# A recurrence's outputs in one run of products per half, and four transfers that the planner treats as independent

## The chip, the cores and the metric

One core of a Trainium2 chip. The time is that of one execution of the whole program in microseconds on the device; the figure of a kernel is the median of its runs. A core has four compute engines that the profile names PE (matrix products; PEld are its weight loads), DVE, ACT and POOL, and SP, which only issues transfers here. They run on their own and meet at semaphores.

## The reference, cut to what matters

A block of an encoder over 1024 positions of width 1024, in float32: a normalised input goes through one wide projection `h @ w_in`, whose columns feed two branches (stick-breaking attention and an RWKV-7 recurrence), then sigmoid gates, an output projection, and a SwiGLU FFN. The change lies in the recurrence. For each of 8 heads of 64 channels it is

```python
def step(state, inp):
    r_t, w_t, k_t, v_t, kk_t, a_t = inp
    sa = jnp.einsum('bhvk,bhk->bhv', state, -kk_t)
    state = (state * w_t[:, :, None, :]
             + sa[..., None] * (kk_t * a_t)[:, :, None, :]
             + v_t[..., None] * k_t[:, :, None, :])
    return state, jnp.einsum('bhvk,bhk->bhv', state, r_t)
```

over the positions, and its outputs `y` are normalised per head, get a bonus term and are gated.

## The kernel before, in words

**Tiling.** The recurrence works on pairs of heads (4 pairs, 128 rows: one head in rows 0 to 63, the other in 64 to 127) and on halves of 512 positions, so there are eight (pair, half) units. A half is cut into 8 chunks of 64 positions. `rw_elementwise` makes what each chunk needs: `ar` (decayed keys and queries), `bk`, and `nx`, two tiles of four chunks each that hold products of `bk` and `ar` under a mask; these are the 64-row products `e_e<-b_ar,b_bk`. `rw_inverse` inverts the triangular part of all chunks of a half at once: DVE works off 31 steps of forward substitution in tile `ts` (class `q`), then four transfers write every fourth row of `ts` to a DRAM scratch `td` (lines 1033 and 1034), one transfer reads `td` back in another order (`dt`, line 1036), and 32-row products on PE finish it. `rw_chain` walks through the 8 chunks: a product with `nx` and the state `sv` (tile `c`, `c_c<-b_sv,b_nx`), two copies into `xv`, a product with `bkt` (`c_c<-b_xv,b_bkt`), and two operations that make the next state in `sv`. After chunk 3 and after chunk 7 it makes the outputs of the four chunks past: 8 products of 64 rows and 64 columns (`y_y<-b_ar,b_sv`) and 8 of 128 rows and 64 columns (`y_y<-b_nx,b_xv`) into one PSUM tile `y`. `rw_post` copies `y` out, normalises, gates and stores it.

**What else PE has meanwhile.** The projections of the next pair (`project`) and the sigmoid gates (`gate_tiles`), 128-row products into tile `d` (`d_d<-big_h,whi_whi` and `d_d<-big_h,wlo_wlo`); the gates come with the lowest priority, wherever there is room. After the recurrence come attention, the merge, the output projection and the FFN, which are products of full size.

**The order.** No line issues an instruction directly. Every operation is recorded with a priority (its place in the program, moved by offsets: the chain comes 1000 places ahead, the inverse 300, gates 10 million behind) and with the operations that it depends on, found from overlapping regions. A planner, `schedule`, then plays the program through with estimated costs (`cost`) and latencies (`LATENCY`: 2030 ns from one transfer to an operation that needs it) and writes out one fixed order for each engine. In it:

- `choose` picks PE's next operation among those that are ready. Normally that is the one of highest priority; after a product whose cost is under 70 it takes another of cost under 70 if one is ready. `array_mode` gives a product's share of the PE array: its contraction rows and its columns, each rounded up to 32, 64 or 128.
- `together()` makes products a bundle, which is issued in one piece once all of its operations can go.
- Tiles lie in pools with a fixed number of places: `y` has 2 places of PSUM, `c`, `d` and `e` 2 each, `b` 27 places in SBUF. A tile takes a place when the planner grants it and gives it back after its last reader.
- Two transfers to the same DRAM tensor whose regions seem to overlap depend on each other for the planner. The regions of the four `td` transfers interleave, and `regions` describes them by their outer span.

All instructions are issued at line 579, so the profile's rows are told apart by their tiles.

## Time and profile before

| | |
|---|---|
| median of 3 runs | 1610.81 us (1609.73 to 1612.65) |
| profiled execution | 1610.57 us, span 1608.8 us |
| PE busy | 1586.0 us, 99% of the span |
| DVE, ACT, POOL busy | 1128.0, 716.5, 254.5 us |
| granted PE clock | 0.999 |
| recurrence's first and last `td` transfer | 152.9 and 463.4 us |
| recurrence's first and last output product | 185.9 and 507.9 us or just after |

The span is the time from the first to the last instruction; the execution's own time has some work around it besides. Rows of groups read: engine, operation, tile written and tiles read, shape, count, busy time, mean ns of one, idle time of the engine before them. Rows in order of time read: start, length, engine, operation, tiles, shape, count, and in brackets the engine's idle time and what ended it. Rows of waits read: who waited for whom, us in total, times, the longest. Matmuls are pipelined: their lengths overlap, and what one costs is the distance between starts.

### The profile page before, as it was taken

To read this page: it belongs to the slowest core of one execution; us is meant where nothing else is said; L and a number is where in the kernel's file an instruction comes from. 1 tells how busy PE (TensorE), PEld (TensorE's weight loads), DVE (VectorE), ACT (ScalarE), POOL (GpSimd) and SP (SyncE) were. 2 spreads that over 40 slices of the span, in tenths; PEclk is the share of its full clock that TensorE was granted. 3 is DMA by queue.
4 is the path that set the end of the run, shared out by engine and by line. 5 is a ranking of instruction groups with operands and counts; after the bars stand their busy time and mean duration, and the time that the engine had idled before them with its cause. 6 is when DMAs were issued, how large, how long until landed. Compare 5 with 4: busy or idle time off the path is not lost.

```text
span 1608.8 us, 23912 instructions
## 1 busy us (share of the span) xinstructions
PE 1586.0 (99%) x8932; PEld 1284.1 (80%) x8932; DVE 1128.0 (70%) x2004; ACT 716.5 (45%) x1401; POOL 254.5 (16%) x407
## 2 busy tenths in 40 slices
PE   9999999999999999999999999999999999999998
PEld 7877777777787888888787888888888888888876
DVE  7568689897864878895366349766666666867485
ACT  7533345444245766774444334323332332554352
POOL 1030233525233222230043110000000000000000
PEclk9999999999999999999999999999999999999999
DMA  5523233242321000003537112332232233874444
GB/s 214 203 88 92 79 100 86 59 140 83 105 71 40 27 27 27 27 27 122 180 118 274 66 40 81 116 98 98 99 111 89 95 111 124 310 240 144 136 152 183
DMA packets 106822, 180.38 MB, mean 112 GB/s; under 512 B 42321, under 2 KB 43345, under 8 KB 106706
## 3 DMA queue, kind: packets, MB, share of 16 engines
q1 hardware_dynamic: 106706, 178.85, 33.6%
q8 instruction: 70, 1.15, 0.3%
q14 instruction: 46, 0.38, 0.1%
HBM read 129.27 MB, written 47.45 MB: 110 GB/s over the span
## 4 chain that ended last, share of the span: by engine, by line
PE 86%; DVE 7%; ACT 3%; DMA 3%; issue 1%; POOL 0%; SPq 0%; DVEq 0%; ACTq 0%; POOLq 0%
PE d_d L579 39%; PE e_e L579 20%; PE c_c L579 16%; PE y_y L579 10%; DVE q_q L579 2%; DVE b_sv L579 1%; DMA b_wraw<-w_fd 0%; DVE big_h L579 0%; DVE b_xs L579 0%; ACT b_qst L579 0%; DMA q_q<-td 0%; DVE wlo_wlo L579 0%; DMA whi_oraw<-w_o 0%; DMA b_g<-gsc 0%; DVE b_nx L579 0%
## 5 line engine op out<-in xcount | busy, mean ns | idle before, releaser
L579 PE MATMUL d_d<-big_h,whi_whi 128*128 128x512 f32 x1280 | 434.5, 409 | 0.1
L579 PEld LDWEIGHTS d_d<-big_h,whi_whi 128*128 128x128 f32 x1280 | 234.9, 189 | 48.7 <-issue 5.5
L579 PE MATMUL d_d<-big_h,wlo_wlo 128*128 128x512 f32 x640 | 259.9, 406 | 0.0
L579 PEld LDWEIGHTS d_d<-big_h,wlo_wlo 128*128 128x128 f32 x640 | 120.7, 189 | 24.6 <-issue 2.4
L579 DVE TENSOR_TENSOR q_q<-b_nl,q_q 128x2 f32<-128x2 f32 (+30 forms) x248 | 86.5, 349 | 9.9 <-POOL b_sh L579 2.4
L579 ACT CAST whi_whi<-raw_raw 128x1024 fp32r<-128x1024 f32 (+1 forms) x60 | 55.9, 933 | 77.5 <-PE d_d L579 76.4
L579 DVE TENSOR_TENSOR_SCAN b_nb<-b_nb 128x128 f32<-128x128 f32 (+3 forms) x64 | 87.9, 1390 | 1.7 <-POOL b_nb L579 1.0
L579 DVE TENSOR_TENSOR wlo_wlo<-raw_raw,whi_whi 128x1024 fp32r<-128x1024 f32 (+1 forms) x60 | 69.5, 1160 | 27.4 <-ACT whi_whi L579 27.3
L579 POOL TENSOR_SCALAR sp_sp<-b_sv,pl_pl 64x64 f32<-64x64 f32 x120 | 63.3, 528 | 121.9 <-DVE b_sv L579 115.9
L579 ACT CAST b_wd<-b_wraw 128x512 fp32r<-128x512 f32 x70 | 42.1, 620 | 64.4 <-DVE b_wraw L579 30.0
L579 DVE TENSOR_REDUCE q_q<-q_q 128x1 f32<-128x2 f32 (+30 forms) x248 | 62.1, 250 | 6.8
L579 PE MATMUL d_d<-b_wd,big_act 128*128 128x512 f32 x264 | 66.5, 395 | 0.0
L579 PE MATMUL e_e<-b_wd,big_act 128*128 128x512 f32 x264 | 66.5, 394 | 0.0
L579 DVE TENSOR_TENSOR b_wd<-b_wraw,b_wd 128x512 fp32r<-128x512 f32 x70 | 46.4, 686 | 27.0 <-ACT b_wd L579 27.0
L579 POOL TENSOR_SCALAR_AFFINE_SELECT b_nb<-b_nb 128x128 f32<-128x128 f32 x64 | 45.4, 716 | 123.5 <-ACT b_nb L579 108.4
L579 PEld LDWEIGHTS e_e<-b_wd,big_act 128*128 128x128 f32 x264 | 49.6, 188 | 11.8
L579 PEld LDWEIGHTS d_d<-b_wd,big_act 128*128 128x128 f32 x264 | 49.6, 188 | 11.7
L579 DVE TENSOR_TENSOR b_wt<-c_c,b_wt 128x512 fp32r<-128x512 f32 (+2 forms) x96 | 50.0, 546 | 3.8 <-ACT b_wt L579 2.7
L579 ACT CAST b_wt<-c_c 128x512 fp32r<-128x512 f32 (+2 forms) x96 | 43.5, 481 | 20.5 <-PE c_c L579 19.5
L579 ACT COPY b_xv<-c_c 64x64 f32<-64x64 f32 x64 | 13.3, 207 | 86.2 <-DVE b_xv L579 46.0
L579 PE MATMUL c_c<-b_wd,big_act 128*128 128x512 f32 x198 | 50.8, 395 | 0.1
L579 PE MATMUL y_y<-b_wd,big_act 128*128 128x512 f32 x198 | 50.7, 394 | 0.0
(648 smaller groups left out, 3576.4 us busy)
## 6 DMA issues: line engine op xcount, KB each, us to landing
raw_raw<-w_in SPq DMA_DIRECT2D x42, 512.0 KB, 3.5
raw_raw<-w_fg SPq DMA_DIRECT2D x22, 512.0 KB, 3.5
raw_raw<-w_fu SPq DMA_DIRECT2D x22, 512.0 KB, 3.6
b_wraw<-w_fd SPq DMA_DIRECT2D x22, 512.0 KB, 4.7
act<-b_u SPq DMA_DIRECT2D x39, 256.0 KB, 3.1
b_x<-x SPq DMA_DIRECT2D x16, 512.0 KB, 9.0
b_mg<-gsc SPq DMA_DIRECT2D x28, 256.0 KB, 5.3
raw_araw<-act SPq DMA_DIRECT2D x14, 512.0 KB, 4.5
```

Of the source, the lines that this page charges most:

```text
L579: getattr(getattr(self.real, op.engine), op.method)(**kw)
```

## The change

Three edits. (1) `choose`: the rule "after a short one, another short one" goes by the array's contraction rows (under 128) in place of the estimated cost (under 70). (2) `rw_inverse`: the four transfers to `td` are taken out of each other's dependencies; the read of `td` still depends on all four. (3) `rw_chain`: the outputs of all eight chunks of a half are made in one bundle behind the last chunk (16 products of the one kind, then 16 of the other), where there were two bundles of 8 and 8, behind chunk 3 and chunk 7.

```diff
-        if able[0][2].engine == "tensor" and last is not None and last.cost < 70:
-            short = [x for x in able if x[2].cost < 70]
+        if able[0][2].engine == "tensor" and last is not None and array_mode(last)[0] < P:
+            short = [x for x in able if array_mode(x[2])[0] < P]
...
     td = b.scratch([32, 8, 4, 32], f"td{p}{hf}")
+    stores = set()
     for c in range(4):
         nc.sync.dma_start(td[:, :, c, :], ts[c:P:4])
+        b.ops[-1].preds -= stores
+        stores.add(b.ops[-1])
...
-        if c % 4 == 3:
-            g = c // 4
-            if y is None:
-                y = u["y"] = T("y", [P, H])
-            with b.together():
-                for k in range(4 * g, c + 1):
-                    for h, rs in hs:
-                        nc.tensor.matmul(y[rs, k * CH : k * CH + CH], lhsT=sv[rs, k, rs], rhs=ar[rs, k, CH:P], start=k == 0, stop=False, skip_group_check=True)
-                for k in range(4 * g, c + 1):
-                    for h, rs in hs:
-                        nc.tensor.matmul(y[rs, k * CH : k * CH + CH], lhsT=xv[:, k, rs], rhs=nx[g][:, k % 4, 1, h, :], start=False, stop=k == 7, skip_group_check=True)
+    y = u["y"] = T("y", [P, H])
+    with b.together():
+        for k in range(8):
+            for h, rs in hs:
+                nc.tensor.matmul(y[rs, k * CH : k * CH + CH], lhsT=sv[rs, k, rs], rhs=ar[rs, k, CH:P], start=k == 0, stop=False, skip_group_check=True)
+        for k in range(8):
+            for h, rs in hs:
+                nc.tensor.matmul(y[rs, k * CH : k * CH + CH], lhsT=xv[:, k, rs], rhs=nx[k // 4][:, k % 4, 1, h, :], start=False, stop=k == 7, skip_group_check=True)
```

## The prediction

> **What bounds the kernel now.** First the head of the page, its busy times and the engines' shares of the chain that ended last.

> ```profile
> span 1608.8 us, 23912 instructions
> ## 1 busy us (share of the span) xinstructions
> PE 1586.0 (99%) x8932; PEld 1284.1 (80%) x8932; DVE 1128.0 (70%) x2004; ACT 716.5 (45%) x1401; POOL 254.5 (16%) x407
> ...
> PE 86%; DVE 7%; ACT 3%; DMA 3%; issue 1%; POOL 0%; SPq 0%; DVEq 0%; ACTq 0%; POOLq 0%
> ```

> PE has work for 1586.0 of 1608.8 us and makes 86% of the chain. So a gain has to come out of PE's own stream: fewer products, less time lost between them, or fewer waits of PE. A result that is ready sooner on another engine is worth nothing unless PE stood waiting for it. Second, two stretches side by side: the recurrence (130 to 520) and the dense stretch of the FFN (960 to 1400).

> ```profile
> core 0: us, PE busy (x) PEld busy (x) DVE busy (x) ACT busy (x) POOL busy (x), PEclk, DMA share, GB/s
> 130.00:520.00 390.00, 384.02 (x3218) 303.75 (x3217) 308.95 (x833) 162.91 (x354) 126.92 (x239) 1.00 0.30 86
> 960.00:1400.00 440.00, 440.00 (x1906) 356.88 (x1905) 304.70 (x454) 146.64 (x234) 0.00 (x0) 1.00 0.34 115
> ```

> In the recurrence PE is without work for 390.00 - 384.02 = 6.0 us. The change touches nothing after it, and the granted clock is 1.00 in both. Third, what PE waited for there, the two largest rows:

> ```profile
> PE c_c L579 <- DVE b_sv L579: 2.2, 5, 0.7
> PE c_c L579 <- ACT b_xv L579: 1.4, 3, 0.6
> ```

> Both are steps of the serial chain over the chunks, and short (0.7 us at most). Otherwise projections and gates (tile d) fill PE while the chain, the inverse or a transfer is under way. That fill is the cover for everything below that I cost at nothing.

> **The outputs of a half in one run.** No product is added or removed; two runs of 16 products become one of 32, and one run's changes of array shape go. Fourth view: PE in order of time around a first run (start, length, operation, count), and the groups by shape.

> ```profile
> 184.19 0.38 PE L579 MATMUL c_c<-b_sv,b_nx 128*128 128x128 f32 x2
> 184.33 0.71 PE L579 MATMUL d_d<-big_h,whi_whi 128*128 128x512 f32 x2
> 184.88 0.39 PE L579 MATMUL d_d<-big_h,wlo_wlo 128*128 128x512 f32 x1
> 185.11 0.63 PE L579 MATMUL d_d<-big_h,whi_whi 128*128 128x512 f32 x2
> 185.58 0.38 PE L579 MATMUL c_c<-b_xv,b_bkt 128*128 128x128 f32 x2
> 185.89 0.68 PE L579 MATMUL y_y<-b_ar,b_sv 64*64 64x64 f32 x16
> 186.50 0.69 PE L579 MATMUL y_y<-b_nx,b_xv 128*64 128x64 f32 x16
> 187.12 0.50 PE L579 MATMUL d_d<-big_h,wlo_wlo 128*128 128x512 f32 x1
> 187.46 0.38 PE L579 MATMUL c_c<-b_sv,b_nx 128*128 128x128 f32 x2
> ```
> ```profile
> L579 PE MATMUL y_y<-b_nx,b_xv 128*64 128x64 f32 x256 | 11.0, 228 | 0.0
> L579 PE MATMUL y_y<-b_ar,b_sv 64*64 64x64 f32 x256 | 10.9, 224 | 0.0
> L579 PE MATMUL e_e<-b_ar,b_bk 64*128 64x128 f32 x192 | 13.9, 285 | 0.0
> ```

> A float32 product stands as two passes: 256 passes of each kind in runs of 16 are 16 runs, two for each of the eight halves. Starts are read, since lengths overlap.
> - From the chain's product at 185.58 to the next one at 187.46 pass 1.88 us: that product, the run, one d product.
> - Without the run: c to d takes 184.33 - 184.19 = 0.14. The d product after a c takes 0.55 (184.33 to 184.88, two of them) less the usual 0.23 (184.88 to 185.11) = 0.32. Together 0.46.
> - So a run costs 1.88 - 0.46 = 1.42 us.
> - Its pace: 16 passes of one kind take 0.68 from first start to last end and one lasts 0.224, so 15 steps take 0.456, 0.030 each. Sixteen more passes are 0.49 us, both kinds 0.97.
> - Doubling one run therefore costs 0.97 and saves the other's 1.42: 0.45 a half, over eight halves **3.6 us off PE's stream**.

> I take 3.6. Every first run has whole-array work on both sides in the trace, so no change of shape was shared there. [...]

> [...]

> What moves with it: the outputs of chunks 0 to 3 leave their place ahead of chunk 4's first product, which can start up to 1.4 us sooner, and come instead ahead of the next half's first product and of the normalisation, about 1.0 us later there. Fill covers both; without that cover it is eight times the difference, about 3 us either way. On POOL, DVE, ACT and SP nothing is added.

> Held longer: the first nx tile of the "b" pool (27 places), now until the second run's time. Held shorter: the y place. In the same half the second run begins 12.3 us after the first (185.89 to 198.19), and the copy that frees y comes just behind it:

> ```profile
> 198.19 0.68 PE L579 MATMUL y_y<-b_ar,b_sv 64*64 64x64 f32 x16
> 198.80 0.69 PE L579 MATMUL y_y<-b_nx,b_xv 128*64 128x64 f32 x16
> ```
> ```profile
> 199.61 0.59 ACT L579 COPY b_gg<-y_y 128x512 f32<-128x512 f32 x1 [1.96 <-POOL b_ar L579]
> ```

> So y is held for 14.3 us (185.89 to 200.20) now and for some 3 us after; the next half's inverse has both y places to itself meanwhile. I put this at nothing: PE's waits name neither place.

> **The choice of the next product.** After a product with under 128 contraction rows the planner now takes another such one; so far this was after products with an estimate under 70. Outputs end in a 128-row product (128*64 above) and lose the rule; the 64*128 products (192 passes, 12 runs here) gain it. Lost: at three places the outputs are followed directly by another run of part-array products, two of them of this form:

> ```profile
> 389.97 0.69 PE L579 MATMUL y_y<-b_nx,b_xv 128*64 128x64 f32 x16
> 390.58 0.33 PE L579 MATMUL y_y<-b_bkt,b_tmp 64*64 64x64 f32 x4
> ```

> A neighbour saves an exit (187.12 to 187.46 is 0.34 against 0.23: 0.11) and an entry (185.58 to 185.89 is 0.31 against 0.14: 0.17), 0.28 us. So the loss is at most 0.8. The gain is at most 12 x 0.28 = 3.4, if after every 64*128 run another is ready. I take 0: ready neighbours are rare, and the gain and loss are of a size.

> **The four stores.** SyncE's issues around one inverse, and around the one where nothing stood between:

> ```profile
> 340.72 1.22 SPq L579 DMA_DIRECT2D td<-q_q  x2
> 343.60 0.33 SPq L579 DMA_DIRECT2D orw<-b_ptmp  x1
> 344.99 0.33 SPq L579 DMA_DIRECT2D gsc<-b_tmp  x1
> 345.36 0.52 SPq L579 DMA_DIRECT2D td<-q_q  x1
> 347.79 0.33 SPq L579 DMA_DIRECT2D raw_raw<-w_in  x1
> 348.17 0.52 SPq L579 DMA_DIRECT2D td<-q_q  x1
> ...
> 351.55 0.37 SPq L579 DMA_DIRECT2D q_q<-td  x1
> ```
> ```profile
> 460.53 3.45 SPq L579 DMA_DIRECT2D td<-q_q  x4
> ```
> ```profile
> DMA to landing us min/median/max: 1.9/2.4/3.9
> ```

> On the chip the stores never waited for each other (two in 1.22 us, four in 3.45): what the planner took for a dependence only spread them over the queue, behind stores that wait for POOL or ACT and a weight load that waits for its buffer. In one row they take 4 x 0.6 = 2.4 us, plus a landing of 2.4, so the read goes out 4.8 us after the first store instead of 351.55 - 340.72 = 10.8: about 6 us sooner, eight times. What they move past on SP (weight loads, gate and output stores) is issued up to 1.8 us later. ACT's cast of the weights covers that:

> ```profile
> ACT whi_whi L579 <- PE d_d L579: 31.5, 15, 6.7
> ```

> It waits for PE to give a buffer back, not for the load. Late next after the inverse is the chain, under PE's fill. I put the stores at 0; the bounds are a loss of 1.8 us for one load laid bare and a gain of the 6.0 us that PE stands idle.

> **Sum.** 1610.57 (the profiled execution, 1.8 over its span and 0.24 under the median of the runs) - 3.6 + 0 + 0 = 1607.0, or 1607.2 on the median's scale.

> **Rivals.**
> - *The plan gives it back.* Every priority is renumbered and the four stores have new times, so the order changes over the whole recurrence; 3.6 us is five or six waits of 0.6 us. For: the chain's waits depend on what happens to stand in front on DVE, which is 79% busy there (308.95 of 390). Against: inverses that end sooner leave the planner more room, not less. Time 1609.5 to 1612, about 1610.6.
> - *PE's waits go too.* If inverses 6 us sooner and a free y place let the plan keep chain and fill apart, the 6.0 us of idle PE vanish: 1607.2 - 6.0 = 1601.2; half of them, 1604.2. Against: the waits named are on DVE and ACT in the chain, which no store feeds. [...]
> - *Slower: the nx place.* One place of 27 stays taken for 12.3 us more in each half. If the pool is full then, a projection's output gets no place, its PSUM tile is not drained and the fill stops. For: the pool holds nearly everything of the recurrence. Against: the page has 0.1 us of idle time before the d products of most gates and projections (the last number of the row).

> ```profile
> L579 PE MATMUL d_d<-big_h,whi_whi 128*128 128x512 f32 x1280 | 434.5, 409 | 0.1
> ```

>   One such hold laid bare costs 12.3: 1607.2 + 12.3 = 1619.5. It decides the sign from 3.6 us on, and a measurable loss from 6.8 us, 1614.0.

> **How the numbers follow.** A measurement of this kernel tells 0.2% (3.2 us) from no change: faster is below 1607.6, slower above 1614.0. The sum as it stands gets 0.45, with a range of its own from 1605.5 to 1609; some six in ten of it lie below 1607.6. The plan gives it back 0.23; waits go too 0.18 (of which the reading by weight loads 0.03); the nx place 0.14. So faster 0.28 + 0.18 = 0.46, same 0.17 + 0.23 = 0.40, slower 0.14. The range runs from 1602.0, into the second rival, to 1613.0, over the first; it leaves out the slower case and the lowest part of the second, 0.19.

> **What would show it.** Right: eight runs of 32 and 32 passes of outputs, each about 2.4 us from first start to the next product, and none with 16; q_q<-td issued about 5 us after the first td; PE's idle time between 130 and 520 still near 6 us; the stretch from the merge on as long as before. Wrong: PE waits on b_sv, b_xv or q_q that sum to 3 us more or less than now, a d product that waits, or a gap at the end of attention, where the planner's order could also differ.

## The result and the profile after

The changed kernel takes 1614.74 us (median of 14 runs, 1610.9 to 1620.07) against 1610.87 us (14 runs, 1608.89 to 1613.04) before: ratio 1.0023, 95% interval 1.0015 to 1.0031. It is 3.9 us slower where 3.6 us of gain were forecast. The profiled execution took 1613.99 us. The head of its page and the engines' shares of the chain:

```profile
span 1612.2 us, 23902 instructions
## 1 busy us (share of the span) xinstructions
PE 1586.4 (98%) x8932; PEld 1281.9 (80%) x8932; DVE 1125.0 (70%) x2004; ACT 715.8 (44%) x1401; POOL 258.3 (16%) x407
...
PE 83%; DVE 8%; DMA 3%; issue 2%; ACT 1%; POOL 1%; SPq 0%; DVEq 0%; POOLq 0%; ACTq 0%
```

PE has the same 1586 us of work, and 3.4 us more of span around it. The two stretches of the prediction:

```profile
core 0: us, PE busy (x) PEld busy (x) DVE busy (x) ACT busy (x) POOL busy (x), PEclk, DMA share, GB/s
130.00:520.00 390.00, 380.50 (x3195) 297.17 (x3195) 304.64 (x830) 162.18 (x351) 132.32 (x239) 1.00 0.30 85
960.00:1400.00 440.00, 440.00 (x1905) 356.62 (x1904) 303.71 (x453) 147.49 (x236) 1.45 (x1) 1.00 0.33 114
```

In the recurrence PE stands without work for 390.00 - 380.50 = 9.5 us, where it was 6.0. The dense stretch is unchanged: from the first product of the merge to the end both traces take 848.9 us (759.9 to 1608.8, and 763.3 to 1612.2). What PE waited for between 130 and 530, all rows:

```profile
PE y_y L579 <- DVE q_q L579: 5.2, 5, 1.4
PE e_e L579 <- DVE b_nx L579: 1.8, 4, 0.8
PE c_c L579 <- ACT b_xv L579: 0.9, 1, 0.9
PE c_c L579 <- DVE b_xv L579: 0.8, 2, 0.4
```

The chain's waits on b_sv (2.2 us before) are gone. In their place PE waits 5.2 us in five places, up to 1.4 us each, for DVE to hand it the transposed read of `td`: the first 32-row run of an inverse. In the kernel before, that row was

```profile
PE y_y L579 <- DVE q_q L579: 1.0, 2, 0.7
```

The waits on q_q come from the inverse's transfers, which got *faster*. Here is one inverse, SyncE's issues and DVE's transpose behind them:

```profile
337.10 2.53 SPq L579 DMA_DIRECT2D td<-q_q  x4
339.73 0.55 SPq L579 DMA_DIRECT2D gsc<-b_tmp  x1
343.17 0.38 SPq L579 DMA_DIRECT2D q_q<-td  x1
```
```profile
345.56 0.45 DVE L579 STREAM_TRANSPOSE q_q<-q_q 128x256 f32<-128x256 f32 x1 [2.02 <-DMA q_q<-td]
```

The four stores go in 2.53 us and the transpose starts 345.56 - 337.10 = 8.5 us after the first. In the kernel before it was 355.68 - 340.72 = 15.0 us at the same inverse:

```profile
355.68 0.44 DVE L579 STREAM_TRANSPOSE q_q<-q_q 128x256 f32<-128x256 f32 x1
```

But the planner counts 0.45 us for each store and 2.03 until it has landed, and gives the transpose 6.8 us after the first store (from 332.35 to 339.13 in its own plan). Over the eight inverses the changed plan puts it 6.4 to 7.1 us behind the first store, and on the chip it starts between 0.2 us sooner and 1.7 us later than that, 0.7 us later in the mean. In the kernel before the plan had 12.5 to 14.3 us, and the chip was between 0.4 us sooner and 0.8 us later. PE's order is fixed by the plan, and PE in order of time shows what follows:

```profile
344.27 0.40 PE L579 MATMUL d_d<-big_h,wlo_wlo 128*128 128x512 f32 x1
346.07 0.69 PE L579 MATMUL y_y<-q_q,b_nx 32*32 32x32 f32 x32 [1.40 <-DVE q_q L579]
346.69 0.81 PE L579 MATMUL d_d<-big_h,whi_whi 128*128 128x512 f32 x2
347.30 0.63 PE L579 MATMUL d_d<-big_h,wlo_wlo 128*128 128x512 f32 x1
347.73 0.63 PE L579 MATMUL d_d<-big_h,whi_whi 128*128 128x512 f32 x1
348.15 0.63 PE L579 MATMUL c_c<-b_sv,b_nx 128*128 128x128 f32 x2
```

The products behind the 32-row run belong to the same tile d, and read the same kinds of operands, as those ahead of it. They could have gone first, but the order puts them behind, and PE waits 1.40 us. Then a second cost: the d products behind it last 0.63 us, 0.43 apart (347.30 to 347.73), not 0.39 and 0.23. The windows around it give the granted clock:

```profile
343.80:347.20 3.40, 2.00 (x38) 1.43 (x37) 1.55 (x2) 2.17 (x4) 1.12 (x1) 1.00 0.45 116
347.20:350.60 3.40, 3.40 (x10) 2.73 (x10) 1.06 (x3) 1.18 (x4) 1.35 (x4) 0.50 0.68 228
350.60:354.00 3.40, 3.40 (x44) 2.57 (x44) 0.33 (x3) 1.07 (x3) 0.00 (x0) 1.00 0.04 17
```

After a stretch in which PE worked 2.00 of 3.40 us, the clock is 0.50 for 3.4 us, which costs half of it, 1.7 us. Over the runs of the changed kernel the mean granted clock goes from 0.999 in the fastest (1610.9 us) to 0.994 in the slowest (1620.1). One such stretch takes 1.7/1612 = 0.001 off the mean, so by this estimate the number of stretches differs from run to run, and with it the time.

The long run of outputs does what it should. PE around the first one, and the groups by shape between 130 and 520:

```profile
191.47 0.41 PE L579 MATMUL c_c<-b_xv,b_bkt 128*128 128x128 f32 x2
191.81 1.15 PE L579 MATMUL y_y<-b_ar,b_sv 64*64 64x64 f32 x32
192.89 1.15 PE L579 MATMUL y_y<-b_nx,b_xv 128*64 128x64 f32 x32
193.97 0.50 PE L579 MATMUL d_d<-big_h,wlo_wlo 128*128 128x512 f32 x1
194.31 0.40 PE L579 MATMUL d_d<-big_h,whi_whi 128*128 128x512 f32 x1
```
```profile
L579 PE MATMUL y_y<-b_nx,b_xv 128*64 128x64 f32 x256 | 9.2, 225 | 0.0
L579 PE MATMUL y_y<-b_ar,b_sv 64*64 64x64 f32 x256 | 9.2, 221 | 0.0
```

From the c product to the d product after the next is 194.31 - 191.47 = 2.84 us; less the 0.46 of the c and d themselves a long run costs 2.38 us, against 2.39 forecast and 2 x 1.42 for two short ones: 3.7 us less over eight halves. So of the 3.4 us of span: 3.7 gained in the outputs, 3.5 lost in idle PE, 1.7 to the half clock, 0.4 before the recurrence (the first 64-row run starts at 110.57 in place of 110.14; the changed kernel's profile has a stretch of half clock at 33.2, that of before has none there). The remaining 1.5 us I cannot assign.

### The profile page after: what moved, and what is told of

Read it like the earlier page. It is cut to its first block, busy times and chain, and to the rows that moved or that the text cites. A ratio compares the mean times of both kernels' runs of the same rounds, so it can differ in the third digit from the quotient of the medians.

```text
span 1612.2 us, 23902 instructions
## 1 busy us (share of the span) xinstructions
PE 1586.4 (98%) x8932; PEld 1281.9 (80%) x8932; DVE 1125.0 (70%) x2004; ACT 715.8 (44%) x1401; POOL 258.3 (16%) x407
## 4 chain that ended last, share of the span: by engine, by line
PE 83%; DVE 8%; DMA 3%; issue 2%; ACT 1%; POOL 1%; SPq 0%; DVEq 0%; POOLq 0%; ACTq 0%
PE d_d L579 37%; PE e_e L579 19%; PE c_c L579 17%; PE y_y L579 11%; DVE q_q L579 3%; DVE b_nx L579 1%; DVE b_sv L579 1%; DVE b_bk L579 1%; DMA b_nl<-nd 1%; DMA q_q<-td 1%; SPq L579 0%; DVE wlo_wlo L579 0%; DMA whi_oraw<-w_o 0%; DMA b_mg<-gsc 0%; DVE big_h L579 0%
## 5 line engine op out<-in xcount | busy, mean ns | idle before, releaser
L579 PE MATMUL d_d<-big_h,whi_whi 128*128 128x512 f32 x1280 | 434.6, 409 | 0.3
L579 PEld LDWEIGHTS d_d<-big_h,whi_whi 128*128 128x128 f32 x1280 | 235.5, 189 | 48.9 <-issue 5.6
L579 PE MATMUL d_d<-big_h,wlo_wlo 128*128 128x512 f32 x640 | 261.8, 409 | 0.0
L579 PEld LDWEIGHTS d_d<-big_h,wlo_wlo 128*128 128x128 f32 x640 | 120.9, 189 | 23.9 <-issue 2.2
L579 DVE TENSOR_TENSOR q_q<-b_nl,q_q 128x2 f32<-128x2 f32 (+30 forms) x248 | 86.7, 350 | 16.8 <-PE y_y L579 7.1
L579 ACT CAST whi_whi<-raw_raw 128x1024 fp32r<-128x1024 f32 (+1 forms) x60 | 55.8, 932 | 85.1 <-PE d_d L579 83.4
L579 DVE TENSOR_TENSOR wlo_wlo<-raw_raw,whi_whi 128x1024 fp32r<-128x1024 f32 (+1 forms) x60 | 68.0, 1134 | 29.9 <-ACT whi_whi L579 29.6
L579 DVE TENSOR_TENSOR_SCAN b_nb<-b_nb 128x128 f32<-128x128 f32 (+3 forms) x64 | 85.2, 1351 | 4.9 <-POOL b_nb L579 4.5
L579 POOL TENSOR_SCALAR sp_sp<-b_sv,pl_pl 64x64 f32<-64x64 f32 x120 | 64.2, 535 | 127.1 <-DVE b_sv L579 121.3
L579 ACT CAST b_wd<-b_wraw 128x512 fp32r<-128x512 f32 x70 | 42.2, 620 | 63.0 <-DVE b_wraw L579 29.3
L579 DVE TENSOR_REDUCE q_q<-q_q 128x1 f32<-128x2 f32 (+30 forms) x248 | 62.1, 250 | 6.8
L579 PE MATMUL e_e<-b_wd,big_act 128*128 128x512 f32 x264 | 66.5, 394 | 0.0
L579 PE MATMUL d_d<-b_wd,big_act 128*128 128x512 f32 x264 | 66.5, 394 | 0.0
L579 DVE TENSOR_TENSOR b_wd<-b_wraw,b_wd 128x512 fp32r<-128x512 f32 x70 | 46.2, 686 | 25.5 <-ACT b_wd L579 25.5
L579 POOL TENSOR_SCALAR_AFFINE_SELECT b_nb<-b_nb 128x128 f32<-128x128 f32 x64 | 41.8, 660 | 124.2 <-ACT b_nb L579 121.7
L579 PEld LDWEIGHTS e_e<-b_wd,big_act 128*128 128x128 f32 x264 | 49.6, 188 | 11.8
L579 PEld LDWEIGHTS d_d<-b_wd,big_act 128*128 128x128 f32 x264 | 49.6, 188 | 11.7
L579 DVE TENSOR_TENSOR b_wt<-c_c,b_wt 128x512 fp32r<-128x512 f32 (+2 forms) x96 | 50.4, 547 | 4.5 <-ACT b_wt L579 3.3
L579 ACT CAST b_wt<-c_c 128x512 fp32r<-128x512 f32 (+2 forms) x96 | 43.8, 480 | 18.6 <-PE c_c L579 17.5
L579 PE MATMUL c_c<-b_wd,big_act 128*128 128x512 f32 x198 | 50.7, 395 | 0.0
L579 PE MATMUL y_y<-b_wd,big_act 128*128 128x512 f32 x198 | 50.7, 394 | 0.0
L579 ACT ACTIVATE b_nb<-e_e 128x512 f32<-128x512 f32 (+2 forms) x96 | 43.4, 496 | 8.3 <-PE e_e L579 6.7
```

What stands on the lines that cost most here:

```text
L579: getattr(getattr(self.real, op.engine), op.method)(**kw)
```

## The experiments

Two theories stood at the start. **Theory 1**: the stores, taken as independent, are planned too early, and PE waits in a fixed order; the long run itself gains its 3.6 us. **Theory 2**: the long run, placed later and holding an nx tile longer, upsets chain and fill. Numbers of `q_q` below are PE's waits on DVE's q_q between 130 and 530. The *planned end* is what the kernel's own planner puts on its last instruction; it is an estimate and no measurement, but the distance from it to the span shows how far the chip differs from the plan.

**The parts one by one.** e1 is the kernel before with the outputs' edit alone, e2 with the stores' edit alone, e3 with the rule of `choose` alone, each as in the diff above.

> The kernel before with the outputs of a half in one run and nothing else of the change. Theory 1 (the stores' new plan leaves PE waiting at the inverse; the longer run itself does what its sum said): output products and the chain's steps into them take 4 to 5 us less, PE waits on q_q stay near the 1.0 us of before, time 1606 to 1608. Theory 2 (the longer run, with its later place and the nx tile held longer, upsets chain and fill): no such gain, PE waits grow by 3 us or more, time 1611 to 1616.

Measured: 1614.73 us, ratio to before 1.0022 (1.0014 to 1.0031), q_q 1.3 us.

> The kernel before with only the four stores taken out of each other's dependencies. Theory 1: the 32-row run of each inverse stands about 1 us too early in PE's order; PE waits on q_q sum to 4 to 6 us, one or more of them followed by a stretch of half clock; time 1614 to 1617. Theory 2: no more waits than before, time 1609 to 1611.

Measured: 1624.25 us, ratio 1.0069 (1.0055 to 1.0084). Its largest wait of PE, and that wait's place in order of time:

```profile
PE y_y L579 <- DVE q_q L579: 4.6, 3, 2.5
```
```profile
206.76 0.40 PE L579 MATMUL d_d<-big_h,wlo_wlo 128*128 128x512 f32 x1
209.71 0.89 PE L579 MATMUL y_y<-q_q,b_nx 32*32 32x32 f32 x32 [2.54 <-DVE q_q L579]
```

> The kernel before with only the rule for PE's next product changed. Both theories: within 1.5 us of before, PE waits as before (about 6 us in the recurrence). A third theory, that the rule pulls products ahead for which PE then waits, expects 1613 or more.

Measured: 1610.17 us, ratio 0.9995 (0.9987 to 1.0004), q_q 0.2 us. In this one order the rule is worth nothing either way.

For the stores, the waits that Theory 1 expects are there: q_q is 4.6 us, and the clock is 0.50 for 3.4 us right behind the 2.54 us wait. The time is far over its range, though: 13 us lost, where 3 to 6 were expected. Part of this loss is in the plan already, since the planned end of e2 is 1603.7 us, 4.7 later than the 1599.1 of before. For the outputs Theory 1 fails: alone they are as slow as the whole change, without its waits on q_q. Theory 2's numbers came (1614.7 us, and idle PE between 130 and 520 grew from 6.0 to 10.9 us), but its cause is not shown: the largest waits are on b_sv, b_xv and b_kst (2.9, 2.0 and 1.8 us), steps of the chain and attention's keys, and no wait for an nx tile's place was found. About half of e1's loss is clock: its mean over the runs is 0.9964 where the kernel before has 0.9976 in the runs beside it, by estimate 0.0012 x 1613 = 2 of the 3.8 us. And the planned end of e1 is 1603.1 us, 4.0 later than that of before: the planner itself found a worse order.

**Only PE's order at the inverse.** e6 leaves the changed kernel's plan alone and moves up to five d products, which the plan has next and whose inputs are written, ahead of the first 32-row run.

```diff
-            for op in self.schedule():
+            for op in fill_first(self.schedule()):   # at each first 32-row run of an inverse: the next
+                                                     # products of tile d whose inputs are written, up to five, go first
```

> The changed kernel with its own plan; only on PE, at each inverse, up to five products of tile d that the plan has next go ahead of the first 32-row run (1.2 us of work; seven of eight inverses have five to move). Theory 1: the waits of 1.3, 1.4, 1.4 and 0.8 us on q_q shrink to 0.3 us or less, the stretch of half clock behind one of them goes; 4 to 6 us under the changed kernel, 1608 to 1611. Theory 2: within 1 us of the changed kernel, 1614 to 1616.

Measured: 1613.81 us, ratio to before 1.0018 (1.0010 to 1.0027), 0.9 us under the changed kernel. Its waits (issue is at line 602 here):

```profile
PE c_c L602 <- ACT b_nx L602: 2.6, 4, 0.7
PE e_e L602 <- DVE b_nx L602: 2.2, 4, 0.9
...
PE y_y L602 <- DVE q_q L602: 0.7, 2, 0.5
```

The 32-row run hardly waits any more (0.7 us in two places), but the chain's first product, which the plan has four d products behind it, now waits for ACT's copy of nx, 0.7 us at four inverses. The half clock did not appear in the recurrence of this profile. Theory 1's gain of 4 to 6 us did not come; the lateness moved one link on. So moving one run is not enough; the next two runs give the planner the later time for everything behind the inverse.

**The price in the plan.** e5 and e8 tell the planner what the traces show. The stores' issues are 0.6 to 0.66 us apart; the transpose starts up to 1.7 us later than planned. The 655 ns are the measured distance. The read's 1000 ns are a cushion and no measured price: the trace has 0.38 us for its issue.

```diff
         b.ops[-1].preds -= stores
         stores.add(b.ops[-1])
+        b.ops[-1].cost = 655.0       # e5 and e8
     dt = T("q", [P, 8, 32])
     nc.sync.dma_start(dt[:], td.rearrange("(c a) j k t -> (a j k) c t", a=4))
+    b.ops[-1].cost = 1000.0          # e8 alone
```

> The changed kernel; the planner counts each of the four stores with 655 ns, the distance of their issues in the traces, in place of 450. The planner's own end is 1599.6 us, 2.4 later than the changed kernel's 1597.2. Theory 1 (part of the loss is a plan that is too optimistic about the inverse's transfers): the distance between the span and the planner's end falls from 15.0 us to 11 to 13, PE waits on q_q from 5.2 us to 2 or less; span 1610.5 to 1612.5, time 1612 to 1614. Theory 2 (what the plan says of the transfers does not matter): the distance stays at 15, time 1616 to 1617.

Measured: 1611.12 us, ratio to before 1.0006 (0.9997 to 1.0015); q_q 2.8 us; span 1608.1, 8.5 over the planned end where the changed kernel has 15.0. All of this goes Theory 1's way, but its numbers were missed: q_q stayed over 2, and time, span and distance came out under their ranges.

> As the kernel with the stores priced, and the read of td counted with 1000 ns in place of 450, because the trace has it 0.6 to 1.7 us later than planned at four of eight inverses. Planner's end 1595.5. Theory 1: PE waits on q_q under 1.5 us, no half clock in the recurrence, span 10 to 12 us over the planned end, time 1607 to 1609.5, under both kernels. Theory 2: distance 15, time 1612 to 1613.

Measured: 1608.29 us, ratio to before 0.9982 (0.9973 to 0.9991): faster than both kernels. Its waits of PE, the two largest, and SyncE at the same inverse:

```profile
PE y_y L579 <- DVE q_q L579: 2.0, 4, 0.9
PE c_c L579 <- DVE b_sv L579: 1.3, 3, 0.8
```
```profile
339.00 2.53 SPq L579 DMA_DIRECT2D td<-q_q  x4
...
343.30 0.37 SPq L579 DMA_DIRECT2D q_q<-td  x1
```

The transfers go as in the changed kernel, four stores in 2.53 us and the read 4.3 us behind the first. What differs is the order that the planner wrote around them. The time is in its range. q_q missed its forecast (2.0, not under 1.5), the distance to the planned end is 12.4 us, a little over the range, and one stretch of half clock remains, at 127.9 us, ahead of the first inverse.

**How much an order is worth by itself.** The planner's margin on a wait between engines is an estimate; a few ns of it mean nothing on the chip but draw another order. e7 does that to e1, e9 to the kernel before.

```diff
-MARGIN = 80
+MARGIN = 79       # e7; 75 in e9
```

> The kernel with the outputs in one run alone (1614.7), and one number that means nothing changed: the planner's margin on a wait between engines is 79 ns in place of 80. Its planned end falls from 1603.1 to 1598.1 us. Theory A (the loss of that kernel is an unlucky order, which any small number changes): span about 10 us over the planned end, time 1609 to 1611. Theory B (the longer run costs what it costs wherever it lands): 1613 to 1616.

Measured: 1610.21 us, ratio to before 1.0002 (0.9993 to 1.0010): 4.5 us under e1.

> A control: the kernel before with nothing of the change, only the margin 75 ns in place of 80. Planner's end 1604.7 in place of 1599.1. Theory A (order alone is worth several us): time 1615 to 1618. Theory B (orders from almost the same numbers cost the same on the chip): 1610 to 1612.

Measured: 1623.98 us, ratio 1.0086 (1.0072 to 1.0099), with nothing of the change in it. Its largest wait, in order of time, is of another kind:

```profile
472.14 0.49 PE L579 MATMUL c_c<-b_sv,b_nx 128*128 128x128 f32 x2
475.18 0.70 PE L579 MATMUL d_d<-big_h,whi_whi 128*128 128x512 f32 x2 [2.55 <-DVE b_kst L579]
```

A projection waits for DVE, which still works on attention's keys (b_kst). The loss is even larger than Theory A expects: order alone is worth several us, and a single order of a part says little. Each version was therefore drawn again at margins 78 and 79: the changed kernel (e10, e11), the priced one of e8 (e12, e13), the kernel before (e14, e15), the outputs alone (e16), the stores alone (e17).

> The changed kernel with the planner's margin 78 ns in place of 80; planner's end 1596.6. Second draw of the changed kernel's order. Theory 1 (the inverse's transfers are planned too early, in any order): PE waits on q_q of 4 us or more again, distance of span to planned end 13 to 17, time 1612 to 1616. Theory A alone (only the luck of the order): distance anywhere from 9 to 20, no tie to q_q, time 1607 to 1618.

> The changed kernel with margin 79 ns; planner's end 1597.8. Third draw. Theory 1: PE waits on q_q of 4 us or more, distance 13 to 17, time 1613 to 1617. Theory A alone: distance 9 to 20.

> The kernel with stores and read priced (1608.3), margin 78 ns; planner's end 1598.5. Theory 1: PE waits on q_q 2 us or less, distance 9 to 13, time 1609 to 1613. Theory A alone: distance 9 to 20, time up to 1620.

> The kernel with stores and read priced, margin 79 ns; planner's end 1597.3. Theory 1: PE waits on q_q 2 us or less, distance 9 to 13, time 1608 to 1612. Theory A alone: distance 9 to 20.

> The kernel before, nothing of the change, margin 78 ns; planner's end 1601.4 in place of 1599.1. Theory A (the kernel before stands on a lucky order; orders drawn by a meaningless nudge are slower on the chip as in the plan): time 1612 to 1617. Theory B: 1610 to 1612.

> The kernel before, margin 79 ns; planner's end 1601.7. Theory A: time 1612 to 1617. Theory B: 1610 to 1612.

> Outputs in one run alone, margin 78 ns; planner's end 1598.2, against 1603.1 at margin 80 (1614.7) and 1598.1 at 79 (1610.2). If the sum's 3.6 us is there beside the luck of the order, the mean over margins 78, 79 and 80 lies 2 to 5 us under that of the kernel before at the same margins; this run 1609 to 1611. If it is not, the two means lie within 1.5 us.

> The four stores alone, margin 79 ns; planner's end 1603.5. Theory 1: PE waits on q_q of 4 us or more, distance of span to planned end 13 to 20, time 1618 to 1624, slower than the kernel before at the same margin. Theory A alone: no such wait, distance 9 to 20.

Measured, medians in us, with the ratio's interval to the kernel before as measured beside them for the new ones:

| margin, ns | 75 | 78 | 79 | 80 |
|---|---|---|---|---|
| before | 1624.0 | 1619.6 (1.0047 to 1.0077) | 1615.1 (1.0025 to 1.0044) | 1610.9 |
| outputs alone | | 1611.1 (0.9998 to 1.0017) | 1610.2 | 1614.7 |
| stores alone | | | 1626.4 (1.0089 to 1.0123) | 1624.3 |
| changed | | 1611.5 (0.9998 to 1.0017) | 1614.5 (1.0007 to 1.0031) | 1614.7 |
| changed, priced | | 1609.4 (0.9984 to 1.0003) | 1608.1 (0.9971 to 0.9990) | 1608.3 |

| | q_q, us | span less planned end, us |
|---|---|---|
| before, margins 75, 78, 79, 80 | 0, 1.5, 2.7, 1.0 | 20.8, 17.0, 14.5, 9.7 |
| outputs alone, 78, 79, 80 | 1.1, 2.0, 1.3 | 11.8, 10.9, 10.2 |
| stores alone, 79, 80 | 6.6, 4.6 | 21.6, 19.4 |
| changed, 78, 79, 80 | 5.3, 4.3, 5.2 | 13.1, 14.1, 15.0 |
| changed and priced, 78, 79, 80 | 1.4, 1.7, 2.0 | 8.2, 9.0, 12.4 |

The waits that separate the versions, from e11 and e17 (stores at 0.45 us) and e13 (priced), all at margin 79:

```profile
PE y_y L579 <- DVE q_q L579: 4.3, 6, 1.9
```
```profile
PE y_y L579 <- DVE q_q L579: 6.6, 6, 2.4
```
```profile
PE y_y L579 <- DVE q_q L579: 1.7, 2, 1.4
```

Three things follow.
- *The stores planned too early are shown.* All five kernels with independent stores at 0.45 us, in the planner's own order, have q_q of 4.3 to 6.6 us; no other has more than 2.8. (e6 moved products by hand and has 0.7.) At the three margins the priced kernel is faster than the changed one by 2.1, 6.4 and 6.4 us, 5.0 in the mean; at margin 80 it is 5.6 when each is set against the kernel before as measured beside it. The profiles account for this: idle PE between 130 and 520 is 9.5, 11.2 and 9.5 us in the changed kernels and 7.2, 6.7 and 5.6 in the priced ones, 3.6 less in the mean, and each changed kernel has one stretch of half clock (1.7 us) behind a q_q wait, the priced ones none (the mean clock of the profiled executions is 0.997 in all three changed kernels and 0.998, 0.998 and 0.997 in the priced ones, the last with its stretch at 127.9 us). Together that is 5.3 us by estimate.
- *The kernel before stands on a lucky order.* Its other three draws are 4 to 13 us slower, and only 2.3 to 5.6 us of that are in their planned ends. The change is compared with the best of four. The means at margins 78, 79 and 80 are 1615.2 before and 1613.6 changed, so against the mean of these draws the changed kernel is no slower. That is three draws of each, and no proof of a gain.
- *The outputs' 3.6 us are shown in the stream, not in the total.* With the outputs alone the mean is 1612.0, 3.2 us under that of before as the sum says; but draws of one version differ by up to 8.7 us, so three of each do not prove it.

The distance to the planned end does not separate the versions: the kernel before at margin 75 has 20.8 with no wait on q_q at all. And several forecasts of these draws were missed: e10 (1611.5) lies half a us under its range, e14 (1619.6) and e17 (1626.4, distance 21.6) lie 2 to 3 us over theirs, e16 is 0.1 over, and the distance of e12 is 8.2 where 9 to 13 was expected. Why the stores cost 13 us alone and much less together with the outputs stays open.

## Why the prediction was wrong

- **The outputs in one run** (3.6 us off PE's stream): right in the mechanism and in size. The long run costs 2.38 us (2.39 forecast), and the outputs' busy time falls from 11.0 and 10.9 to 9.2 and 9.2 us.
- **The choice of the next product** at 0: as forecast in the one order that was drawn; alone 0.9995 (0.9987 to 1.0004).
- **The four stores** at 0, between a loss of 1.8 and a gain of 6.0 us: *this step failed*. The facts in it were right: the stores never waited for each other on the chip (four in 2.53 us now), the read now goes out 4.0 to 6.1 us behind the first (4.8 forecast). The conclusion was wrong: "Late next after the inverse is the chain, under PE's fill." The fill is no pool from which PE takes what is ready; it is a fixed list. Work that stands behind the 32-row run covers nothing while that run waits. The false dependence made the planner put the stores 2.5 us apart, which hid that it counts 0.45 us for an issue that takes 0.6 to 0.66: on the chip the read of `td` then went out up to 1.5 us sooner after the first store than planned, and never more than 0.2 us later. With the dependence gone, the read is up to 2.2 us later than planned, the transpose up to 1.7. The waits on q_q went from 1.0 to 5.2 us, one of them has a stretch of half clock behind it, and higher prices for the transfers give back 5.0 us in the mean.
- **Bounds of the stores**: the loss was bounded by a weight load laid bare, 1.8 us. A better bound was in reach. The trace of before has the stores' issues 0.6 us apart and `cost` says 0.45: by estimate 0.15 us for each of four issues at eight inverses, 4.8 us, where the waits on q_q came to 5.2.
- **A wait's price**: it was taken as its own length. The traces show a second term, 3.4 us at half clock behind some waits of 1.4 us and more: 1.7 us each, in the changed kernel's profile once in the recurrence.
- **The base of the sum**, 1610.57: it was taken as what any order of this kernel takes, but it is the time of one order. Three other orders of the same kernel take 1615.1 to 1624.0. That the comparison fell on the best of the four is luck, and the sign rests on it in part.
- **Rival "the plan gives it back"** (1609.5 to 1612): this is what happened in kind, by both of its halves, but 3 us too small. New orders of the same kernel spread over 13 us, not over the 3 us that the range allowed for.
- **Rival "PE's waits go too"**: the inverse did come sooner (the second half of pair 1 starts its 32-row run at 294.15 in place of 302.32), and the waits on b_sv went. Others took their place. No run shows the reading by weight loads, which holds 0.03 of this rival's chance: between 130 and 520 the weight loads were busy for 303.75 us before and for 297.17 in the changed kernel, and PE's idle time rose from 6.0 to 9.5 us.
- **Rival "slower: the nx place"**: the sign came, the mechanism did not. The b pool's nx tiles appear in PE's waits (1.8 us on b_nx, none in the recurrence before), but at all four of these waits the DVE operation that writes nx (at 225.27, 295.54, 401.57 and 413.32) starts right behind another one: DVE was busy and did not wait for a place. And the outputs alone at margins 78 and 79 are not slower than before.
- **What would show it**: runs of 32 and 32 passes, yes; the read about 5 us behind, yes; the stretch from the merge on as long as before, yes; idle PE near 6 us between 130 and 520, no: 9.5. The sign of being wrong, waits on b_sv, b_xv and q_q 3 us more or less in sum, did not come: 5.0 before, 6.9 now, since q_q rose by 4.2 while b_sv fell by 2.2.

## What to carry to other kernels

Where a planner writes one fixed order, a dependence that the chip does not have can still be useful slack: before it is removed, compare the planner's price of each step in it with the trace, and put the measured price in with the same edit. Fill covers a late operation only where it stands *ahead* of it in that order: PE, busy for 98% of the span, waited up to 1.40 us here with d products right behind. And a version of a planned kernel is one draw: change a number that means nothing by a few ns and measure again before a difference of a few us is put down to an edit.

## What the runs showed of the hardware

The stretches lie on a grid in these two profiles. They begin a whole number of 3.413 us apart: 92 steps in the changed kernel (33.16 and 347.19), and 51, 26 and 59 steps in e2:

```profile
35.92:39.33 3.41, 3.41 (x19) 3.41 (x18) 3.32 (x5) 1.90 (x4) 0.00 (x0) 0.50 0.70 185
210.00:213.41 3.41, 3.41 (x34) 2.86 (x28) 1.87 (x5) 1.71 (x5) 3.17 (x5) 0.50 0.03 9
298.75:302.16 3.41, 3.41 (x18) 2.90 (x17) 2.84 (x6) 0.28 (x2) 2.68 (x3) 0.50 0.10 15
500.14:503.55 3.41, 3.41 (x12) 2.83 (x12) 1.17 (x2) 0.21 (x1) 1.71 (x2) 0.50 0.66 211
```

What decides within a step of the grid is not shown. In the changed kernel PE was busy for 2.01 of the 3.41 us of the step ahead of the half clock, and for 2.07 in the step with the wait at 205.17, which brought none. In the kernel before, PE waited 2.27 us until 126.52 and was busy for only 1.62 of the 3.41 us around that wait, a step counted back in 3.413 us from its stretch at 1606.11, and this brought none either:

```profile
126.52 1.16 PE L579 MATMUL e_e<-cst_cst,b_sg 128*128 128x128 f32 x8 [2.27 <-DVE b_nx L579]
```
```profile
124.73:128.14 3.41, 1.62 (x13) 1.62 (x14) 3.07 (x15) 0.41 (x2) 0.00 (x0) 1.00 0.07 10
128.14:131.56 3.42, 3.42 (x18) 2.80 (x18) 3.01 (x14) 3.36 (x7) 0.00 (x0) 1.00 0.49 80
```

So the busy share alone does not decide.
